# Holding back the first gates' sigmoids with a bias column made from the attention's last exponentials

## The chip, the cores and the metric

The kernel runs on one core of one Trainium2 chip. The metric is device time in microseconds (us), the median of the runs. Before the change it is 992.24 us, over three runs from 991.83 to 992.85 us.

## The reference

One layer of a streaming encoder, for 512 prompt frames and 32 frames of a running stream (544 columns in all, D_MODEL = 1024). What matters here is the stick-breaking attention, the gates, and what joins them:

```python
def stick_breaking_block(q, k, v, q_pos, k_pos):
    z = jnp.einsum('bqhd,bkhd->bhqk', q, k).astype(jnp.float32) * (SB_HEAD_DIM ** -0.5)
    mask = (k_pos[None, :] < q_pos[:, None])[None, None]
    u = jnp.where(mask, jax.nn.log_sigmoid(-z), 0.0)
    after = lax.cumsum(u, axis=3, reverse=True) - u
    w = jnp.where(mask, jnp.exp(jax.nn.log_sigmoid(z) + after), 0.0)
    return jnp.einsum('bhqk,bkhd->bqhd', w.astype(v.dtype), v)

def merge(o_ret, rg, o_sb, ga, gb, ret_norm_w_l, w_out_l):
    B, T = o_ret.shape[:2]
    r = rmsnorm(o_ret, ret_norm_w_l).reshape(B, T, RET_WIDTH).astype(rg.dtype) * jax.nn.silu(rg)
    s = o_sb.reshape(B, T, SB_WIDTH)
    mix = jax.nn.sigmoid(ga) * r + jax.nn.sigmoid(gb) * s
    return mix @ w_out_l
...
# rg, ga, gb are three of the nine parts of h @ w_in, h = rmsnorm(x)
# y = x + merge(...), then y + sq_relu_mlp(rmsnorm(y))
```

There are eight stick-breaking heads and four retention heads. The prompt's attention runs over all 512 frames; the sample's attention reads 512 cached keys and values beside its own 32.

## The kernel before, in words

Everything is held transposed: features on the 128 partitions, the 544 frames along the columns. Each float32 product is three products of rounded halves (hi x hi, lo x hi, hi x lo), made by `products` and `exact`. A projection (`gemm`) is a 128 x 1024 weight tile times the normalised input h, in two halves of 272 columns; a half is 24 matmuls into one PSUM bank of the pool `mm`, which has three banks. At its start `gemm` also calls `load_w`, which fetches the weight tile of the next one and splits it: a cast on ScalarE (ACT) to `whi`, a subtraction on VectorE (DVE) to `wlo`. There are two buffers of each, so the cast waits until the projection before this one has been read out of its weights.

The program first runs the heads in the order of `HEADS`, the last being stick-breaking heads S6 and S7, and then the gates: for each of the eight feature tiles t, the projections rg, ga and gb. Tile 0's three are only copied from PSUM (`first`, three `tmp` tiles). For t = 1 and later the sigmoid of rg is taken straight from PSUM (`silu`), then those of ga and gb. `first_mix`, called after the first projection of t = 1 (the fourth gate tile), takes the sigmoids of tile 0 and mixes it.

Between the matmuls of the projections, TensorE (PE) runs the steps of the attention as they become ready. A planner written in Python (`Flow`) sets PE's order by hand: each chain is a generator (`sb_chain` for a stick-breaking head, `sample_chain` for the cached attention of four heads, and others) that yields what it needs next, and `flow.poll()` between matmuls steps a chain whose inputs are due by the planner's own estimate of ACT's and DVE's time. That estimate holds lengths of operations and nothing for the loading of function tables. Only PE's order is set so (`manual_schedule`); the order on ACT and DVE is chosen by the framework's scheduler from what is ready in its own view.

One stick-breaking head does this: PE makes the scores in three banks (1280 packed columns); ACT takes Abs from PSUM into `e`, then Exp and Ln of `e` in place (softplus); DVE adds max(z, 0) and makes the halves `sh` (hi) and `sl` (lo) of the 1280 columns, then sums later blocks in `e` and makes three more 128-column pieces of `sh` (casts on ACT) and `sl` (DVE), in `later_parts`. PE subtracts the suffix sums from the scores (products of `sh` and `sl` with `tri_r` and `neg1_r`, shown as neg_r); ACT takes Exp of the result into `e`; DVE splits it, and PE multiplies by the values. The sample chain does the same for the sample with a scan on DVE in place of the triangular products; its last exponential is `cum`.

ACT has its functions in table sets, and an ACT_TABLE_LOAD stands in its order where the set changes. The program begins with a set that has both exp and ln. Sigmoid lies in another set. Where the scheduler lets a sigmoid in between two of the attention's functions, a load goes ahead of the sigmoid and another ahead of what follows; as the program is built, an Exp and an Ln that follow a sigmoid get a load each.

Of the kernel before, what the change touches and what calls it, by code (L numbers as in the profile page):

```python
# [9 lines left out]
F32 = mybir.dt.float32  # L10
F32R = mybir.dt.float32r
BF16 = mybir.dt.bfloat16
AF = mybir.ActivationFunctionType
ALU = mybir.AluOpType
# [10 lines left out]
NSB = 8  # L25
# [3 lines left out]
P = 128  # L29
# [3 lines left out]
PACKED = 1280  # L33
# [168 lines left out]
def need(*events, **parts):  # L202
    return events, parts
# [32 lines left out]
def trunk(ctx: ExitStack, tc: tile.TileContext, a: dict, g32):  # L236
    nc = tc.nc
    flow = Flow(mm=3, at=5, tmp=13, e=2, sh=1, qk0=1, qk1=1, qk2=1, qk3=1, vt=2, rv=1, rk=1, rq=1)
    V, S, T = (Timed(e, n, flow) for e, n in ((nc.vector, "V"), (nc.scalar, "S"), (nc.tensor, "T")))
# [97 lines left out]
    nc.vector.tensor_copy(ones_r, ones)  # L337
    ones = ones_r.bitcast(F32)
    ident = cst[:, C_ID:C_MP]
    epsb = const.tile([P, 1], F32, tag="epsb", name="epsb")  # L340
    nc.vector.memset(epsb, EPS)

# [51 lines left out]
    H = (h_hi, h_lo)  # L394
# [311 lines left out]
    def sb_chain(h, vt):  # L706
        yield need(("qk", h, 0), ("qk", h, 1), at=3, e=1)
        q_r, k_r = heads.pop((h, 0)), heads.pop((h, 1))
        z = [bank() for i in range(3)]
        e = bigp.tile([P, PACKED], F32, tag="e", name="e", bufs=2)  # L710
        for i in (0, 2):
            T.matmul(z[i][:, :P], id_b, mp_b, start=True, stop=False, **SG)
        T.matmul(
            z[1].rearrange("p (n c) -> p n c", c=P)[:, ::3, :], id_b,
            mp_b.rearrange("p (o c) -> p o c", o=1).to_broadcast([P, 2, P]), start=True, stop=False, **SG,
        )
        for bi, blocks in enumerate(GROUPS):
            for n, b in enumerate(blocks):
                _, c0, w = PIECES[b]
                by_blocks(z[bi][:, c0 : c0 + w], b, k_r, q_r, False, True)  # L720
        flow.give(qk0=1, qk1=1)
        for bi, (o, w) in enumerate(BANKS):
            S.activation(e[:, o : o + w], z[bi][:, :w], AF.Abs)
        S.activation(e, e, AF.Exp, scale=-1.0)
        S.activation(e, e, AF.Ln, bias=1.0)
        for bi, (o, w) in enumerate(BANKS):
            V.scalar_tensor_tensor(
                e[:, o : o + w], z[bi][:, :w], 0.0, e[:, o : o + w], op0=ALU.max, op1=ALU.add
            )
        yield need(sh=1)  # L730
        parts = packed_parts(e)
        later_parts(e, parts)
        yield need()
        for bi, blocks in enumerate(GROUPS):
            for b in blocks:
                bb, c0, w = PIECES[b]
                o = BANKS[bb][0] + c0
                own, later = z[bi][:, c0 : c0 + w], z[bi][:, c0 + P : c0 + w]
                if b == 3:
                    T.matmul(own, tri, e[:, o : o + w], start=False, stop=True, **SG)  # L740
                    continue
                for s in parts:
                    T.matmul(own, tri_r, s[:, o : o + w], start=False, stop=False, **SG)
                if b == 2:
                    T.matmul(later, neg1, e[:, 896:1024], start=False, stop=True, **SG)
                    continue
                for i, s in enumerate(parts):
                    T.matmul(
                        later.rearrange("p (n c) -> p n c", c=P), neg1_r, spaced(s, (512, 1024)[b], 3 - b),
                        start=False, stop=i == 1, **SG,  # L750
                    )
        flow.give(sh=1)
        for bi, (o, w) in enumerate(BANKS):
            S.activation(e[:, o : o + w], z[bi][:, :w], AF.Exp)
        flow.give(at=3)
        yield need(("v", h), sh=1, at=1)
        parts = packed_parts(e)
        yield need()
        ob = bank()
        values_of(ob, vt, slice(0, P), parts, e)  # L760
        S.copy(s_all[:, h, :SEQ], ob)
        flow.give(at=1, e=1, sh=1, vt=1)
        flow.finish("sb", h)

    def sample_chain(g):

        hs = range(4 * g, 4 * g + 4)
        yield need(*[("qk", h, i) for h in hs for i in range(2)], *[("v", h) for h in hs], tmp=6)
        kc, vc = [], []
        for h in hs:  # L770
            t = tmp()[:, :PAST]
            nc.gpsimd.dma_start(out=t, in_=a["kc"][h])
            kc.append(t)
        flow.t += 8000
        yield need(at=2)
        W0 = HT - DEC
        z = [bank(), bank()]
        T.matmul(z[0][:, :DEC], id_b, ms_b, start=True, stop=False, **SG)
        for j in range(4):
            T.matmul(z[0][j * DEC : (j + 1) * DEC, :DEC], qs[:, j, :], ks[:, j, :], start=False, stop=True, **SG)  # L780
        for j in range(4):
            T.matmul(
                z[0][j * DEC : (j + 1) * DEC, DEC:HT], qs[:, j, :], kc[j][:, :W0], start=False, stop=True, **SG
            )
        for j in range(4):
            T.matmul(z[1][j * DEC : (j + 1) * DEC, :HT], qs[:, j, :], kc[j][:, W0:], start=True, stop=True, **SG)
        for h in hs:
            t = tmp()[:, :PAST].rearrange("p (m e) -> p m e", m=4)
            nc.gpsimd.dma_start(out=t, in_=a["vc"][:, h * P : (h + 1) * P].rearrange("(m p) e -> p m e", p=P))
            vc.append(t)  # L790
        yield need()
        e, cum = tmp(), tmp()
        for i in range(2):
            S.activation(e[:, i * HT : (i + 1) * HT], z[i][:, :HT], AF.Abs)
        S.activation(e, e, AF.Exp, scale=-1.0)
        S.activation(e, e, AF.Ln, bias=1.0)
        for i in range(2):
            c = slice(i * HT, (i + 1) * HT)
            V.scalar_tensor_tensor(e[:, c], z[i][:, :HT], 0.0, e[:, c], op0=ALU.max, op1=ALU.add)
        V.tensor_tensor_scan(cum, ones[:, 0:1].to_broadcast([P, NT]), e, 0.0, op0=ALU.mult, op1=ALU.add)  # L800
        for i in range(2):
            c = slice(i * HT, (i + 1) * HT)
            V.tensor_tensor(cum[:, c], z[i][:, :HT], cum[:, c], op=ALU.subtract)
        flow.give(at=2)
        S.activation(cum, cum, AF.Exp)
        yield need(at=2)
        b = bank()
        for m in range(4):
            T.transpose(b[:, m * P : (m + 1) * P], cum[:, DEC + m * P : DEC + (m + 1) * P], ident)
        b2 = bank()  # L810
        T.transpose(b2[:DEC, :P], cum[:, :DEC], ident)
        wt = tp.tile([P, 4, P], F32, tag="tmp", name="wt")
        wn = sm.tile([DEC, P], F32, tag="wn", name="wn")
        S.copy(wt.rearrange("p m c -> p (m c)"), b)
        S.copy(wn, b2[:DEC, :P])
        flow.give(at=2)
        yield need(at=1)
        ob = bank()
        for m in range(5):
            for j in range(4):  # L820
                o = ob[j * DEC : (j + 1) * DEC, :P]
                if m < 4:
                    T.matmul(
                        o, wt[:, m, j * DEC : (j + 1) * DEC], vc[j][:, m, :], start=(m == 0), stop=False, **SG
                    )
                else:
                    T.matmul(o, wn[:, j * DEC : (j + 1) * DEC], vs[:, j, :], start=False, stop=True, **SG)
        flow.finish("sample", g)
        os_ = sm.tile([P, P], F32, tag="os", name="os")
        S.copy(os_, ob[:, :P])  # L830
        flow.give(at=1, tmp=6)
        yield need(at=1)
        b = bank()
        T.transpose(b[:, :P], os_, ident)
        V.tensor_copy(s_all[:, 4 * g : 4 * g + 4, SEQ:], b[:, :P].rearrange("p (h i) -> p h i", h=4))
        flow.give(at=1)
# [244 lines left out]
    def first_mix():  # L1081
        flow.wait(tmp=1)
        g, sa, sb = first
        sg = tmp()
        S.activation(sg, g, AF.Sigmoid)
        V.tensor_tensor(g, g, sg, op=ALU.mult)
        S.activation(sa, sa, AF.Sigmoid)
        V.tensor_tensor(g, g, sa, op=ALU.mult)
        V.tensor_tensor(g, g, r_all[:, 0, :], op=ALU.mult)
        S.activation(sb, sb, AF.Sigmoid)  # L1090
        V.tensor_tensor(sb, sb, s_all[:, 0, :], op=ALU.mult)
        V.tensor_tensor(g, g, sb, op=ALU.add)
        flow.give(tmp=3)
        held.append((0, g))

    for t in range(1, KD):
# [4 lines left out]
            S.activation(sg[:, c], p, AF.Sigmoid)  # L1101
            V.tensor_tensor(g[:, c], p, sg[:, c], op=ALU.mult)

        gemm(H, silu)
        flow.give(tmp=1)
        if t == 1:
            first_mix()
        flow.wait(tmp=1)
        sa = tmp()
        gemm(H, lambda h, c, p: S.activation(sa[:, c], p, AF.Sigmoid))  # L1110
# [397 lines left out]
```

## Time and profile before

| | |
|---|---|
| median of three runs | 992.24 us (991.83 to 992.85) |
| the profiled execution's own time | 993.84 us |
| its span in the trace | 992.1 us |
| PE busy | 982.7 us, 99% of the span |
| DVE busy | 667.6 us, 67% |
| ACT busy | 534.3 us, 54%, of which 13 ACT_TABLE_LOADs of 1.283 us |
| chain of waits that ended last | PE 97%, ACT 1%, DMA 1%, DVE 1% |

The span is the time between the first and the last instruction that the profiler saw; the execution's own time is 1.7 us more. Times of rows below are microseconds from the span's start. A matmul's duration in the trace overlaps the next one's: what one costs on PE is the distance from its start to the start of the next.

### The profile page before, as it was taken

The numbers are of one execution on the slowest core, as the hardware profiler recorded it, in microseconds if no ns is written. First come the engines' busy times: TensorE is split into PE (matmuls) and PEld (weight loads), VectorE is DVE, ScalarE is ACT, GpSimd is POOL, SyncE is SP. The second block draws the span as 40 slices with busy tenths as digits, with TensorE's granted clock in tenths as the row PEclk, the third lists the DMA queues.
The fourth block names the chain that finished last, engine by engine and source line by source line (L and its number), as shares of the span: only waits on it lengthen the run. The fifth ranks groups of instructions, "written<-read, shape, count | busy, mean of one in ns | idle before, by whom it ended". The sixth has DMA issues, their size and how long they took to land.

```text
span 992.1 us, 18727 instructions
## 1 busy us (share of the span) xinstructions
PE 982.7 (99%) x7766; PEld 968.9 (98%) x7766; DVE 667.6 (67%) x1127; ACT 534.3 (54%) x984; POOL 45.7 (5%) x80
## 2 busy tenths in 40 slices
PE   9999999999999999999999999999999999999998
PEld 9999999999999999988999999999999999999998
DVE  7987874787577756656644357975676666676782
ACT  6457554855576456777433345765464454444440
POOL 0001000120010001110000011000000000000000
PEclk9999999999999999999999999999999999999999
DMA  6233222352133212432422245232323323332312
GB/s 236 92 111 107 98 69 70 110 171 81 39 129 108 64 47 105 134 103 89 133 96 89 86 164 165 92 102 86 106 90 104 106 87 107 93 123 97 120 47 88
DMA packets 30933, 102.73 MB, mean 104 GB/s; under 512 B 4096, under 2 KB 6144, under 8 KB 30848
## 3 DMA queue, kind: packets, MB, share of 16 engines
q1 hardware_dynamic: 24768, 80.88, 25.1%
q0 software_dynamic: 6080, 20.65, 6.1%
q8 instruction: 61, 1.00, 0.4%
q14 instruction: 24, 0.20, 0.1%
HBM read 90.51 MB, written 11.01 MB: 102 GB/s over the span
## 4 chain that ended last, share of the span: by engine, by line
PE 97%; ACT 1%; DMA 1%; DVE 1%; issue 0%; SPq 0%; ACTq 0%; DVEq 0%
PE mm L229 71%; PE at L229 26%; DMA x<-in_x 1%; ACT L229 0%; ACT e L229 0%; ACT whi L229 0%; ACT tmp L229 0%; PE at L614 0%; DVE sl L229 0%; DVE tmp L229 0%; DVE wlo L229 0%; DVE e L229 0%; DVE sh L229 0%; ACT sh L229 0%; DVE x L229 0%
## 5 line engine op out<-in xcount | busy, mean ns | idle before, releaser
L229 PE MATMUL mm<-h_hi,whi 128*128 128x272 f32 x1040 | 303.4, 292 | 0.0
L229 PE MATMUL mm<-h_hi,wlo 128*128 128x272 f32 x1040 | 300.2, 289 | 0.0
L229 PE MATMUL mm<-h_lo,whi 128*128 128x272 f32 x1040 | 299.6, 288 | 0.0
L229 DVE TENSOR_TENSOR wlo<-raw,whi 128x1024 fp32r<-128x1024 f32 (+1 forms) x146 | 167.7, 1150 | 121.7 <-ACT whi L229 121.4
L229 ACT CAST whi<-raw 128x1024 fp32r<-128x1024 f32 (+1 forms) x146 | 144.6, 991 | 178.5 <-PE mm L229 158.2
L229 PEld LDWEIGHTS mm<-h_hi,whi 128*128 128x128 f32 x1040 | 196.1, 189 | 1.1 <-issue 0.6
L229 PEld LDWEIGHTS mm<-h_lo,whi 128*128 128x128 f32 x1040 | 196.2, 189 | 0.2
L229 PEld LDWEIGHTS mm<-h_hi,wlo 128*128 128x128 f32 x1040 | 195.6, 188 | 0.0
L229 PE MATMUL mm<-u_hi,whi 128*128 128x272 f32 x512 | 147.8, 289 | 0.0
L229 PE MATMUL mm<-u_lo,whi 128*128 128x272 f32 x512 | 147.7, 288 | 0.0
L229 PE MATMUL mm<-u_hi,wlo 128*128 128x272 f32 x512 | 147.6, 288 | 0.0
L229 PEld LDWEIGHTS mm<-u_hi,whi 128*128 128x128 f32 x512 | 96.5, 188 | 0.4 <-DVE y L229 0.2
L229 PEld LDWEIGHTS mm<-u_lo,whi 128*128 128x128 f32 x512 | 96.4, 188 | 0.0
L229 PEld LDWEIGHTS mm<-u_hi,wlo 128*128 128x128 f32 x512 | 96.2, 188 | 0.0
L229 ACT ACTIVATE tmp<-tmp 128x544 f32<-128x544 f32 (+2 forms) x157 | 80.6, 558 | 27.5 <-DVE tmp L229 27.0
L229 PE MATMUL at<-f_hi,wlo 128*128 128x272 f32 x320 | 92.6, 289 | 0.0
L229 PE MATMUL at<-f_lo,whi 128*128 128x272 f32 x320 | 92.1, 288 | 0.0
L229 PE MATMUL at<-f_hi,whi 128*128 128x272 f32 x320 | 92.1, 288 | 0.0
L229 DVE TENSOR_TENSOR y<-mm,y 128x272 f32<-128x272 f32 x112 | 48.7, 437 | 29.4 <-PE mm L229 29.4
L229 PEld LDWEIGHTS at<-f_hi,whi 128*128 128x128 f32 x320 | 60.5, 189 | 0.0
L229 PEld LDWEIGHTS at<-f_lo,whi 128*128 128x128 f32 x320 | 60.3, 188 | 0.0
L229 PEld LDWEIGHTS at<-f_hi,wlo 128*128 128x128 f32 x320 | 60.3, 188 | 0.0
(244 smaller groups left out, 1808.8 us busy)
## 6 DMA issues: line engine op xcount, KB each, us to landing
raw<-in_w SPq DMA_DIRECT2D x142, 512.0 KB, 3.5
x<-in_x SPq DMA_DIRECT2D x8, 272.0 KB, 6.0
o_v<-tmp POOLq DMA_DIRECT2D x8, 272.0 KB, 2.4
o_k<-tmp POOLq DMA_DIRECT2D x8, 272.0 KB, 2.4
x<-in_x POOLq DMA_DIRECT2D x8, 272.0 KB, 5.1
o_y<-x POOLq DMA_DIRECT2D x8, 272.0 KB, 2.9
tmp<-o_y POOLq DMA_DIRECT2D x8, 272.0 KB, 4.5
o_y<-y SPq DMA_DIRECT2D x16, 136.0 KB, 1.7
```

What stands on the lines that cost most here:

```text
L229: f(out, *args, **kw)
```

## The change

A const tile `late` of three columns is added. The last head's final exponentials (`e`) and the second sample chain's final exponential (`cum`) are each followed by a one-column DVE operation that multiplies a column of them by zero (columns 0 and 1 of `late`). `first_mix` and a new branch for t = 1 use column 2, the sum of both, as the bias of four sigmoids: it adds zero to what they compute, and makes them wait for both exponentials. For t = 1 the first projection, the fourth gate tile, is copied from PSUM and not put through the sigmoid there; the sigmoid is then taken from the copy over all 544 columns.

```diff
@@ -753,6 +755,9 @@
         for bi, (o, w) in enumerate(BANKS):
             S.activation(e[:, o : o + w], z[bi][:, :w], AF.Exp)
         flow.give(at=3)
+        if h == NSB - 1:
+            V.tensor_scalar(late[:, 0:1], e[:, PACKED - 1 :], 0.0, None, op0=ALU.mult)
+            flow.finish("late", 0)
         yield need(("v", h), sh=1, at=1)
         parts = packed_parts(e)
         yield need()
@@ -803,6 +808,9 @@
             V.tensor_tensor(cum[:, c], z[i][:, :HT], cum[:, c], op=ALU.subtract)
         flow.give(at=2)
         S.activation(cum, cum, AF.Exp)
+        if g == 1:
+            V.tensor_scalar(late[:, 1:2], cum[:, 0:1], 0.0, None, op0=ALU.mult)
+            flow.finish("late", 1)
         yield need(at=2)
         b = bank()
         for m in range(4):
@@ -1082,12 +1090,12 @@
         flow.wait(tmp=1)
         g, sa, sb = first
         sg = tmp()
-        S.activation(sg, g, AF.Sigmoid)
+        S.activation(sg, g, AF.Sigmoid, bias=late[:, 2:3])
         V.tensor_tensor(g, g, sg, op=ALU.mult)
-        S.activation(sa, sa, AF.Sigmoid)
+        S.activation(sa, sa, AF.Sigmoid, bias=late[:, 2:3])
         V.tensor_tensor(g, g, sa, op=ALU.mult)
         V.tensor_tensor(g, g, r_all[:, 0, :], op=ALU.mult)
-        S.activation(sb, sb, AF.Sigmoid)
+        S.activation(sb, sb, AF.Sigmoid, bias=late[:, 2:3])
         V.tensor_tensor(sb, sb, s_all[:, 0, :], op=ALU.mult)
         V.tensor_tensor(g, g, sb, op=ALU.add)
         flow.give(tmp=3)
@@ -1101,10 +1109,17 @@
             S.activation(sg[:, c], p, AF.Sigmoid)
             V.tensor_tensor(g[:, c], p, sg[:, c], op=ALU.mult)
 
-        gemm(H, silu)
+        if t == 1:
+            gemm(H, lambda h, c, p: S.copy(g[:, c], p))
+            flow.until("late", 0)
+            flow.until("late", 1)
+            V.tensor_tensor(late[:, 2:3], late[:, 0:1], late[:, 1:2], op=ALU.add)
+            S.activation(sg, g, AF.Sigmoid, bias=late[:, 2:3])
+            V.tensor_tensor(g, g, sg, op=ALU.mult)
+            first_mix()
+        else:
+            gemm(H, silu)
         flow.give(tmp=1)
-        if t == 1:
-            first_mix()
         flow.wait(tmp=1)
         sa = tmp()
         gemm(H, lambda h, c, p: S.activation(sa[:, c], p, AF.Sigmoid))
```

What this does to ACT's order is seen in two places. The first is ACT from the last head's Abs (`e<-at`) through its Exp and Ln (`e<-e`) to the first gates; `tmp<-mm` as COPY is a gate kept as it is, as ACTIVATE a gate's sigmoid, `tmp<-tmp` here a sigmoid of a copied gate, `whi` the cast of a weight tile. Before:

```order
L229 ACTIVATE e<-at 128x512 x2
L229 ACTIVATE e<-at 128x256
L229 ACT_TABLE_LOAD
L229 ACTIVATE e<-e 128x1280
L229 COPY tmp<-mm 128x272
L229 ACT_TABLE_LOAD
L229 ACTIVATE e<-e 128x1280
L229 CAST whi<-raw 128x1024
L229 ACT_TABLE_LOAD
L229 ACTIVATE tmp<-tmp 128x544
L229 ACTIVATE tmp<-mm 128x272
L229 CAST whi<-raw 128x1024
```

The same place of ACT in the changed kernel, on to the three casts of `sh`:

```order
L229 ACTIVATE e<-at 128x512 x2
L229 ACTIVATE e<-at 128x256
L229 ACTIVATE e<-e 128x1280 x2
L229 CAST whi<-raw 128x1024
L229 COPY tmp<-mm 128x272 x2
L229 CAST sh<-e 128x128
L229 CAST whi<-raw 128x1024
L229 CAST sh<-e 128x128 x2
L229 ACTIVATE tmp<-at 128x272 x2
L229 COPY tmp<-mm 128x272
```

The three loads are gone, Exp and Ln follow each other, and the sigmoids have become copies.

The second place is ACT a little later, where the sample's Exp and Ln (`tmp<-tmp` between the `sh` casts and after), the last head's final Exp (`e<-at`) and the sample's last Exp stand among sigmoids. Before, from the first `sh` cast:

```order
L229 CAST sh<-e 128x128
L229 ACT_TABLE_LOAD
L229 ACTIVATE tmp<-tmp 128x544
L229 CAST sh<-e 128x128 x2
L229 ACT_TABLE_LOAD
L229 ACTIVATE tmp<-tmp 128x544
L229 ACT_TABLE_LOAD
L229 ACTIVATE e<-at 128x512
L229 ACT_TABLE_LOAD
L229 ACTIVATE tmp<-tmp 128x544
L229 ACT_TABLE_LOAD
L229 ACTIVATE e<-at 128x512
```

In the changed kernel, from the sample's Exp and Ln on:

```order
L229 ACTIVATE tmp<-tmp 128x544 x2
L229 ACTIVATE e<-at 128x512 x2
L229 ACTIVATE e<-at 128x256
L229 ACTIVATE tmp<-tmp 128x544
L229 ACT_TABLE_LOAD
L229 ACTIVATE tmp<-tmp,late 128x544 x4
L229 ACTIVATE tmp<-mm 128x272 x2
L229 CAST whi<-raw 128x1024
```

One load is left, ahead of the four sigmoids that read `late`; over the whole program ACT has four loads where it had thirteen.

The third place is DVE in the changed kernel, from the last two `sl` pieces of the last head to the mixing of the gates (`tmp<-ones_r,tmp` is the sample's scan):

```order
L229 TENSOR_TENSOR sl<-e,sh 128x128 x2
L229 SCALAR_TENSOR_TENSOR tmp<-at,tmp 128x272 x2
L229 SCALAR_TENSOR_TENSOR tmp<-ones_r,tmp 128x544
L229 TENSOR_SCALAR late<-e 128x1
L229 CAST sh<-e 128x1280
L229 TENSOR_TENSOR tmp<-at,tmp 128x272 x2
L229 TENSOR_TENSOR sl<-e,sh 128x1280
L229 TENSOR_SCALAR late<-tmp 128x1
L229 TENSOR_TENSOR late<-late 128x1
L229 TENSOR_TENSOR tmp<-tmp 128x544 x3
```

The three `late` operations are new; before, the mixing of tile 0 was spread between the sample's subtraction and the last head's `sh` and `sl`, and now all of it follows. On PE nothing changes up to the gate projections that follow the last head's triangular products; there the sample's five transposes stand nine matmuls earlier, and the last head's product with the values three matmuls earlier.

## Rows read from the trace of the kernel before

**Rows 1.** The page: busy time of PE with its neighbours, and the shares by engine of the chain that ended last.

```profile
PE 982.7 (99%) x7766; PEld 968.9 (98%) x7766; DVE 667.6 (67%) x1127; ACT 534.3 (54%) x984; POOL 45.7 (5%) x80
...
PE 97%; ACT 1%; DMA 1%; DVE 1%; issue 0%; SPq 0%; ACTq 0%; DVEq 0%
```

**Rows 2.** The view of waits for PE over the whole trace: who was waited for, us in total, how often, the longest. All its five rows.

```profile
PE at L229 <- ACT sh L229: 3.1, 1, 3.1
PE at L388 <- DVE ones_r L337: 1.3, 1, 1.3
PE at L229 <- DVE sl L229: 0.8, 1, 0.8
PE mm L229 <- DVE x L229: 0.3, 1, 0.3
PE mm L229 <- ACT whi L229: 0.2, 1, 0.2
```

**Rows 3.** The timeline of PE around the two waits: start, duration, what, and idle time before it. 441.96 is the fourth gate tile's last matmul, 443.27 the first triangular product of head S7, 451.14 the first matmul of the next projection.

```profile
441.96 0.29 PE L229 MATMUL mm<-h_hi,wlo 128*128 128x272 f32 x1
...
443.27 0.50 PE L229 MATMUL at<-sh,tri_r 128*128 128x512 f32 x1
444.55 0.50 PE L229 MATMUL at<-sl,tri_r 128*128 128x512 f32 x1 [0.78 <-DVE sl L229]
448.12 0.44 PE L229 MATMUL at<-sh,neg_r 128*128 128x384 f32 x1 [3.07 <-ACT sh L229]
448.46 0.69 PE L229 MATMUL at<-sl,neg_r 128*128 128x384 f32 x1
...
451.14 0.57 PE L229 MATMUL mm<-h_hi,whi 128*128 128x272 f32 x1
...
451.94 0.28 PE L229 MATMUL mm<-h_hi,whi 128*128 128x272 f32 x1
```

**Rows 4.** The same products of head S6, before the change, where PE waited for nothing: its first `sh` product, its fourth product, the first matmul of the projection behind, and the fourth instruction from that one.

```profile
417.92 0.40 PE L229 MATMUL at<-sh,tri_r 128*128 128x512 f32 x1
...
418.56 0.34 PE L229 MATMUL at<-sl,neg_r 128*128 128x384 f32 x1
...
419.92 0.37 PE L229 MATMUL mm<-h_hi,whi 128*128 128x272 f32 x1
...
420.37 0.68 PE L229 MATMUL at<-tmp_r,ones_r 128*128 128x272 f32 x4
```

**Rows 5.** The table of stretches, PE alone: stretch, its length, busy time and count, granted clock of TensorE (1.00 is 2.4 GHz, 0.50 is 1.2 GHz), DMA share, GB/s.

```profile
449.00:450.00 1.00, 1.00 (x5) 0.50 0.88 348
...
452.00:453.00 1.00, 1.00 (x10) 1.00 0.00 0
```

**Rows 6.** The timeline of ACT over the last head and the first gates; a row with no names is an ACT_TABLE_LOAD.

```profile
433.76 1.28 ACT L229 ACT_TABLE_LOAD   x1
...
436.65 1.28 ACT L229 ACT_TABLE_LOAD   x1
437.95 1.27 ACT L229 ACTIVATE e<-e 128x1280 f32<-128x1280 f32 x1
...
442.31 1.04 ACT L229 CAST whi<-raw 128x1024 fp32r<-128x1024 f32 x1
...
443.54 0.68 ACT L229 ACTIVATE tmp<-at 128x272 f32<-128x272 f32 x2
445.42 0.30 ACT L229 CAST sh<-e 128x128 fp32r<-128x128 f32 x1 [1.20 <-DVE e L229]
445.74 1.28 ACT L229 ACT_TABLE_LOAD   x1
447.03 0.66 ACT L229 ACTIVATE tmp<-tmp 128x544 f32<-128x544 f32 x1
447.59 0.48 ACT L229 CAST sh<-e 128x128 fp32r<-128x128 f32 x2
```

**Rows 7.** The timeline of DVE over the same stretch.

```profile
439.25 1.62 DVE L229 SCALAR_TENSOR_TENSOR e<-at,e 128x512 f32<-128x512 f32 x3 [10.65 <-ACT e L229]
440.79 1.22 DVE L229 TENSOR_TENSOR wlo<-raw,whi 128x1024 fp32r<-128x1024 f32 x1
441.92 0.82 DVE L229 CAST sh<-e 128x1280 fp32r<-128x1280 f32 x1
...
443.01 1.48 DVE L229 TENSOR_TENSOR sl<-e,sh 128x1280 fp32r<-128x1280 f32 x1
...
445.04 0.29 DVE L229 TENSOR_TENSOR e<-e 128x128 f32<-128x128 f32 x1
...
445.60 0.42 DVE L229 TENSOR_TENSOR e<-e 128x256 f32<-128x256 f32 x1
...
447.90 0.50 DVE L229 TENSOR_TENSOR sl<-e,sh 128x128 fp32r<-128x128 f32 x2 [0.55 <-ACT sh L229]
450.07 0.79 DVE L229 SCALAR_TENSOR_TENSOR tmp<-at,tmp 128x272 f32<-128x272 f32 x2 [1.67 <-ACT tmp L229]
450.90 1.29 DVE L229 TENSOR_TENSOR_SCAN tmp<-ones_r,tmp 128x544 f32<-128x544 f32 x1
```

**Rows 8.** From the chain that ended last, in order of time: start, us, what. The longest unbroken piece of projection matmuls.

```profile
466.68 109.66 PE mm L229 x872
```

**Rows 9.** One line's instructions: a DVE operation on one column (L565), min/median/max in ns.

```profile
L565 DVE TENSOR_SCALAR nw<-wv x1: 148/148/148, 2.7 to 2.7; 128x1 f32<-128x1 f32 x1
```

More of the change, by code (lines that the diff above doesn't have):

```diff
@@ L339, in trunk @@
     ident = cst[:, C_ID:C_MP]
+    late = const.tile([P, 3], F32, tag="late", name="late")
     epsb = const.tile([P, 1], F32, tag="epsb", name="epsb")
```

## The prediction

> **What bounds the kernel now.** The page first: PE is busy 99% of the span and carries 97% of the chain that ended last [rows 1]. So ACT's table loads are worth only what PE waits for them. The view of waits for PE has five rows, 5.7 us in all, and 3.9 of these are two waits [rows 2]. The timeline of PE puts both in one place, the triangular products of the last head, S7: the second product waits 0.78 us for DVE's `sl`, the third 3.07 us for ACT's `sh` casts [rows 3]. The other three waits (1.3, 0.3, 0.2 us) lie elsewhere and the change does not touch them.
>
> Behind the wait PE is slow as well. From 449 to 450 us the granted clock is 0.50, 1.2 GHz, and after 452 it is 1.00 again [rows 5]; the fall comes after a stretch of nearly 4.9 us, 443.27 to 448.12, in which PE ran two products [rows 3]. What the place costs is read best by start times. From S7's first product to the fourth projection matmul it is 451.94 - 443.27 = 8.67 us [rows 3]. For head S6, which waited for nothing, the same instructions take 420.37 - 417.92 = 2.45 us [rows 4]. So 6.22 us are lost there: by comparing 448.46 to 451.94 (3.48 us) with S6's 418.56 to 420.37 (1.81 us), 1.67 of them behind the fourth product's start to the slow clock, the rest nearly all to waiting.
>
> **What made PE wait.** ACT's timeline shows it [rows 6]. S7's Abs is done at 433.76. A load stands before Exp and another before Ln (433.76 and 436.65), with a copy of a gate in between, so Ln ends at 439.22; DVE then begins its max-add at 439.25 after an idle time of 10.65 us for which ACT is named [rows 7]. Later a third load (445.74) and the sample's Exp (447.03) stand between the first `sh` cast and the other two, and PE's third product starts 0.05 us after these end.
>
> **The change, part by part.** On ACT the order has 4 loads where it had 13; nine of 1.28 us are 11.5 us of ACT, nearly all of it off the path. Each step on the path I take again in the new order, with durations of before. PE's order is the same up to here, so 443.27 stands.
>
> 1. Exp and Ln follow each other from 433.76: two times 1.27 to 1.28 us, Ln ends at 436.3 instead of 439.2, 2.9 us earlier (two loads and the copy).
> 2. DVE's three max-adds then run 436.35 to 438.0 (1.62 us). The weight tile's `wlo` stands next; its cast runs on ACT from 436.3 and is done before DVE is free; 1.22 us, with the overlap of the row 1.13, so the cast of `sh` starts at 439.0. It takes 0.82, `sl` 1.48: `sl` is ready at 441.4. PE wants it at 443.50 (0.23 behind the first product, as in S6's rows: four products from 417.92 to 418.56). The wait of 0.78 us is gone.
> 3. DVE's adds of 128 and 256 columns (0.29, 0.42 us) end at 442.05 [rows 7]; the first `sh` cast runs on ACT by 442.05 as well.
> 4. Next on ACT, ahead of the other two `sh` casts, now stands the weight cast of the projection behind. It overwrites the weights of the fourth gate tile, whose last matmul starts at 441.96 and ends 0.29 later [rows 3]; before, this cast started at 442.31 [rows 6], and it can hardly start sooner now. It takes 1.04; by the rows' overlap the two `sh` casts run 443.26 to 443.74 (0.48). PE could start the third product at 443.73: 0.06 us of waiting in place of 3.07.
> 5. DVE has `wlo` of that same weight tile ahead of the last two `sl`: 443.37, and 1.13 later, 444.50, the two `sl` with 0.50 us. They end at 445.00. PE's fourth product, which could start at 443.97, starts at 445.06 (before, it started 0.06 behind them too: 448.40 and 448.46): 1.09 us. This is what is late next.
>
> So PE waits 1.15 us where it lost 6.22. The clock: the largest idle time left is about a microsecond in place of 0.78 and 3.07 with one product between, and the 0.3 and 0.2 us waits elsewhere cost no clock that I see. I take it that it stays at 1.00, and keep the other case as a rival. **Gain: 6.22 - 1.15 = 5.07 us.**
>
> What the Trainium skill says of a load is larger: "ScalarE: Activation LUTs", section "What ACT_TABLE_LOAD costs", gives 1283 ns and a drain of some 1380 ns for each switch. The first number is this trace's; the drain isn't seen, since Ln starts 0.02 us behind its load [rows 6]. By the page the two loads of step 1 would give back 5.3 us and not 2.6: Ln would end at 433.9, although it and Exp need 2.5 us from 433.76 on. The rows decide, and the sum above holds no drain.
>
> **What the change adds.** Three one-column operations on DVE: not in the trace in this place; the nearest row is 148 ns on one column [rows 9], the far end is the longest operation of that stretch, the scan with 1.29 us [rows 7]; below nothing is excluded, they are new work. I take 0.15 us. They matter only through the four sigmoids, which wait for their sum on ACT's in-order queue. Behind these four stand the sigmoid of the next projection's first half, which frees a PSUM bank, then a weight cast. From step 5 on: the sample's Abs, the copy of the fourth gate's second half and Exp and Ln end on ACT at about 446.0 (0.68; 0.4 for 272 columns, about half of the two Abs; two of 0.66); DVE's max-add 0.79, scan 1.29, one column, `sh` cast 0.82 and subtraction 0.79 end at 449.8; the last Exp at 450.5, the one load that is left at 451.8. The column sum stands on DVE behind `sl` (1.48) and one more small operation: 451.5, hidden by the load. Four sigmoids of 0.66 end at 454.5, that half's sigmoid takes 0.4, and the bank is free at 454.9. PE starts the next projection at 445.06 + (419.92 - 418.56) = 446.42, and wants that bank three halves later, the earliest at 446.42 + 72 x 0.1258 = 455.5 (109.66 us for 872 matmuls [rows 8]). So it is covered, by 0.6 us. If the small operations cost 1.29 us each the column comes at 455.0, the bank at 458.0, and PE waits 2.5 us: gain 2.6.
>
> The mixing of tile 0 ends later on DVE, but what it feeds is only read after all the gates, and the `tmp` tiles that the sample's cached values load into were released long before. Behind this place PE has 109.66 us without a break [rows 8] and loses nothing that was gained.
>
> The sum is made against the profiled execution: 993.84 - 5.07 = 988.77 us. That execution is 1.60 us above the median of its runs, 992.24; I forecast the median: 992.24 - 5.07 = **987.2 us**.
>
> **The rivals.**
>
> - *The clock falls all the same* (0.11). Against it: the idle time left is a third of the longest one before. For it: the trace shows one fall only, so it doesn't tell how little idle time is enough. Then the slow stretch costs about the 1.67 us that it cost behind the fourth product: gain 3.4, 988.8 us.
> - *The wait vanishes altogether* (0.06), if DVE or ACT gets to the last pieces sooner than step 4 and 5 say: gain 6.2, 986.0 us. Against it: the weight cast cannot start before PE has read the old weights.
> - *Nothing is won, since something else than the loads made PE wait* (0.07): the `sh` casts were late because of DVE's work between, and PE finds another late input: within 2 us of 992. For it: of the 9.15 us from the max-add to the last `sl` before (439.25 to 448.40) my steps still hold 8.65. Against it: both ends move with Ln's 2.9 us, and PE's products come at a fixed 443.27.
> - *Slower* (0.04): the four held sigmoids keep the PSUM bank. It decides from 455.5 on; every microsecond later is one lost, and the kernel is slower than before once the bank comes after 460.6, that is if DVE's queue from Ln to the column sum takes 11.2 us instead of 5.5. With 13.5 us the bank comes at 462.9, PE waits 7.4, and the time is 992.24 - 5.07 + 7.4 = 994.6 us. Against it: before, the same work from the sample's max-add on was never waited for.
>
> **How the numbers follow.** My own case has 0.72, at 986.6 to 987.9 us by 0.3 us in each of steps 4 and 5 and what the runs scatter. With the clock's case at 988.8 and the dear small operations at 989.7 above, and the vanished wait at 986.0 below, the range is 985.9 to 989.7. About 0.2%, 2 us, is what a measurement of this kernel can tell from no change. Faster by more than that: 0.72 + 0.11 + 0.06 = 0.89. Within it: 0.07. Slower: 0.04.
>
> **What the new profile would show.** Right: four ACT_TABLE_LOADs, none between S7's Abs and its Exp and Ln; DVE's max-add at about 436.3; no wait of PE for S7's second product, and one of about 1 us, for `sl` and not for `sh`, at the fourth; the next projection at 446.4 instead of 451.1, at a clock of 1.00; no wait for a PSUM bank near 455. Wrong: a clock of 0.50 behind S7's products, a wait of PE on an ACT sigmoid, or a max-add that starts as late as before although the loads are gone.

## The result and the profile after

The changed kernel takes 986.76 us, the median of four runs from 986.35 to 987.61. The kernel before took 992.04 us beside it (four runs, 991.74 to 992.85). The medians differ by 5.28 us. The ratio on record is 0.9942, with a 95% interval of 0.9929 to 0.9954 (the two medians alone give 0.9947). Of all runs behind this document one, of the kernel below in which the fourth gate tile isn't kept, took 1356.21 us at a mean granted clock of 0.657, and the ratios leave it out. The profiled execution's own time is 986.62 us, its span 984.9 us.

On the page, where [rows 1] stood before, ACT has lost 11 us of work and PE 3.8:

```profile
PE 978.9 (99%) x7766; PEld 965.6 (98%) x7766; DVE 667.8 (68%) x1129; ACT 523.3 (53%) x976; POOL 45.9 (5%) x80
...
PE 99%; DMA 0%; ACT 0%; DVE 0%; issue 0%; SPq 0%
```

The view of waits for PE, all its rows, answers to [rows 2]. The 3.1 us for `sh` is gone; one wait of 0.7 us for `sl` is left.

```profile
PE at L390 <- DVE ones_r L337: 1.3, 1, 1.3
PE at L229 <- DVE sl L229: 0.7, 1, 0.7
PE mm L229 <- ACT whi L229: 0.2, 1, 0.2
```

The timeline of PE at head S7's triangular products answers to [rows 3]. The columns are start, duration, what, and the idle time before it; the last line is the fourth matmul of the next projection.

```profile
441.89 0.50 PE L229 MATMUL at<-sh,tri_r 128*128 128x512 f32 x1
442.23 0.40 PE L229 MATMUL at<-sl,tri_r 128*128 128x512 f32 x1
442.46 0.34 PE L229 MATMUL at<-sh,neg_r 128*128 128x384 f32 x1
443.55 0.44 PE L229 MATMUL at<-sl,neg_r 128*128 128x384 f32 x1 [0.74 <-DVE sl L229]
...
445.02 0.37 PE L229 MATMUL mm<-h_hi,whi 128*128 128x272 f32 x1
...
445.48 0.29 PE L229 MATMUL mm<-h_hi,whi 128*128 128x272 f32 x1
```

From the first product to the fourth projection matmul this is 445.48 - 441.89 = 3.59 us, against 8.67 before: **5.08 us won in this place**. 3.53 of these are waiting ahead of the fourth product (448.46 - 443.27 = 5.19 us before, 1.66 now); the other 1.55 lie behind its start (3.48 us before, 1.93 now), where the clock was slow before. The first product itself starts 1.38 us earlier in this execution than in the one before, and that has nothing to do with the change (the last section has more on it). So the two profiled executions, 993.84 and 986.62, differ by 7.22 us: 5.08 here, 1.38 ahead of here, 0.54 at the wait on `x` that this execution did not have (three starts from 585.23 to 586.03 us before, the same three from 578.60 to 578.86 now), and some 0.2 that gathers slowly over the projections between, without a wait. The medians, which even out much of such chance, differ by 5.28.

ACT's timeline answers to [rows 6]. Exp and Ln are one row (x2), and one load stands behind the sample's last Exp, ahead of the four held sigmoids (`tmp<-tmp,late`):

```profile
432.40 2.58 ACT L229 ACTIVATE e<-e 128x1280 f32<-128x1280 f32 x2
...
440.79 1.05 ACT L229 CAST whi<-raw 128x1024 fp32r<-128x1024 f32 x1
441.74 0.49 ACT L229 CAST sh<-e 128x128 fp32r<-128x128 f32 x2
...
447.99 0.66 ACT L229 ACTIVATE tmp<-tmp 128x544 f32<-128x544 f32 x1 [1.82 <-DVE tmp L229]
448.67 1.28 ACT L229 ACT_TABLE_LOAD   x1
449.96 2.67 ACT L229 ACTIVATE tmp<-tmp,late 128x544 f32<-128x544 f32 x4
452.54 0.66 ACT L229 ACTIVATE tmp<-mm 128x272 f32<-128x272 f32 x2
```

DVE's timeline answers to [rows 7]. The max-add no longer waits 10.65 us but 7.74, and the one-column operations are the short rows with `late`:

```profile
435.01 1.62 DVE L229 SCALAR_TENSOR_TENSOR e<-at,e 128x512 f32<-128x512 f32 x3 [7.74 <-ACT e L229]
...
438.53 1.49 DVE L229 TENSOR_TENSOR sl<-e,sh 128x1280 fp32r<-128x1280 f32 x1
...
441.86 1.23 DVE L229 TENSOR_TENSOR wlo<-raw,whi 128x1024 fp32r<-128x1024 f32 x1 [0.80 <-ACT whi L229]
443.00 0.48 DVE L229 TENSOR_TENSOR sl<-e,sh 128x128 fp32r<-128x128 f32 x2
...
446.40 0.13 DVE L229 TENSOR_SCALAR late<-e 128x1 f32<-128x1 f32 x1
...
449.45 0.16 DVE L229 TENSOR_TENSOR late<-late 128x1 f32<-128x1 f32 x1
```

What is left of the wait reads straight off: DVE's `wlo` starts when ACT's `whi` is done, the last two `sl` stand behind it and start at 443.00, and PE's fourth product starts at 443.55.

### The profile page after: what moved, and what is told of

It reads as the page before. It is cut to its first block, busy times and chain, and to the rows that moved or that the text cites. A ratio compares the mean times of both kernels' runs of the same rounds, so it can differ in the third digit from the quotient of the medians.

```text
span 984.9 us, 18722 instructions
## 1 busy us (share of the span) xinstructions
PE 978.9 (99%) x7766; PEld 965.6 (98%) x7766; DVE 667.8 (68%) x1129; ACT 523.3 (53%) x976; POOL 45.9 (5%) x80
## 4 chain that ended last, share of the span: by engine, by line
PE 99%; DMA 0%; ACT 0%; DVE 0%; issue 0%; SPq 0%
PE mm L229 73%; PE at L229 26%; DMA x<-in_x 0%; ACT whi L229 0%; PE at L616 0%; ACT tmp L229 0%; DVE sl L229 0%; DVE y L229 0%; DVE wlo L229 0%; SPq L332 0%
## 5 line engine op out<-in xcount | busy, mean ns | idle before, releaser
L229 ACT ACTIVATE tmp<-tmp 128x544 f32<-128x544 f32 (+2 forms) x154 | 78.6, 556 | 29.2 <-DVE tmp L229 28.7
```

The source lines that it names most:

```text
L229: f(out, *args, **kw)
```

## The experiments

The theory: the gain is the two loads between S7's Abs, Exp and Ln and the third one between its `sh` casts, which PE waited for, and the slow clock behind that wait. The rivals: it is the gates' own work on ACT and DVE that got out of the way, whatever the loads; or any part of the change (the copies, the columns) does it alone. The first four kernels ran on one chip, beside the kernel before at 993.05 us there; the last three on one chip too, with the kernel before at 992.92.

**One sigmoid put back.** A one-column sigmoid before the last head's Abs makes Exp and Ln follow a sigmoid again. Its one-column result is overwritten by the Abs. Where an expectation speaks of S7's stretch, it means the time from S7's first product to the fourth projection matmul.

```diff
         flow.give(qk0=1, qk1=1)
+        if h == NSB - 1:
+            S.activation(e[:, 0:1], q_r[0][:, 0:1].bitcast(F32), AF.Sigmoid)
         for bi, (o, w) in enumerate(BANKS):
             S.activation(e[:, o : o + w], z[bi][:, :w], AF.Abs)
```

> The changed kernel with one more instruction: a sigmoid of a single column, ahead of the last head's Abs. The gates' sigmoids stay held back, but ACT's order has again a load before S7's Exp, one before its Ln, and one before the sample's Exp, between the sh casts. If the loads made PE wait (the loads' theory): Ln ends about 2.9 us later than in the changed kernel, PE waits about 0.8 us at S7's second product, 3 us at the third, and from S7's first product to the fourth projection matmul 8 to 8.7 us pass instead of 3.6; 4.5 to 5 us slower than the changed kernel, some 991.5 us, if the clock falls as it did before, and about 990 us if it doesn't. If it was the gates' own work on ACT and DVE in that stretch (the rival), which stays away here: within 1 us of 986.8.

Measured: 992.56 us (991.39 to 993.39, 11 runs), ratio to the kernel before 0.9997 (0.9988 to 1.0006). The whole gain is gone, and the median lies 1 us above what was expected. ACT's timeline of this kernel has the three loads in their old places, though the gates' sigmoids are still held:

```profile
432.47 1.28 ACT L229 ACT_TABLE_LOAD   x1
433.76 1.28 ACT L229 ACTIVATE e<-e 128x1280 f32<-128x1280 f32 x1
435.37 1.28 ACT L229 ACT_TABLE_LOAD   x1
...
443.41 0.30 ACT L229 CAST sh<-e 128x128 fp32r<-128x128 f32 x1 [1.20 <-DVE e L229]
...
444.29 1.28 ACT L229 ACT_TABLE_LOAD   x1
445.59 0.66 ACT L229 ACTIVATE tmp<-tmp 128x544 f32<-128x544 f32 x1
446.15 0.48 ACT L229 CAST sh<-e 128x128 fp32r<-128x128 f32 x2
```

PE's timeline has both waits, and the table of stretches for PE (stretch, length, busy time and count, granted clock, DMA share, GB/s) the slow clock behind them:

```profile
441.98 0.50 PE L229 MATMUL at<-sh,tri_r 128*128 128x512 f32 x1
443.05 0.49 PE L229 MATMUL at<-sl,tri_r 128*128 128x512 f32 x1 [0.57 <-DVE sl L229]
446.68 0.69 PE L229 MATMUL at<-sh,neg_r 128*128 128x384 f32 x1 [3.14 <-ACT sh L229]
...
450.26 0.29 PE L229 MATMUL mm<-h_hi,whi 128*128 128x272 f32 x1
```

```profile
448.00:449.00 1.00, 1.00 (x7) 0.50 0.00 0
```

8.28 us from the first product to the fourth projection matmul, 8.67 before and 3.59 in the changed kernel: 4.69 of the 5.08 us are lost again in this place. It is the loads, with the order that comes with them. Three more loads are back as well, ahead of the one-column sigmoid (426.39), of the sample's Ln (446.65) and of the last head's final Exp (448.62). These cost nothing: no wait of PE answers to them, and from the fourth projection matmul to the product that reads `os` (464.35 us here, 459.57 in the changed kernel) 14.09 us pass in both. The edit also moves what the scheduler puts beside the loads (the first `sh` cast is again a row of its own, with the sample's work behind it), as the loads did before, so it doesn't part the loads' own 1.28 us from the order that comes with them.

**The fourth gate tile not kept.** The three sigmoids of tile 0 stay held; the fourth gate tile's is taken from PSUM as before.

```diff
         if t == 1:
-            gemm(H, lambda h, c, p: S.copy(g[:, c], p))
+            gemm(H, silu)
...
-            S.activation(sg, g, AF.Sigmoid, bias=late[:, 2:3])
-            V.tensor_tensor(g, g, sg, op=ALU.mult)
             first_mix()
```

> The bias on the three sigmoids of tile 0 alone; the fourth gate tile is put through its sigmoid straight from PSUM, as before the change. ACT's order keeps S7's Exp and Ln together, but has loads again around the sample's Exp, Ln and last Exp, and a weight cast that waits for PE now stands ahead of the last Exp and the held sigmoids. If only the loads ahead of S7's products counted, and the kept fourth tile is idle: S7's stretch takes 3.6 to 4.0 us and the time is 986.5 to 987.5. If what comes behind counts too: the same stretch, but PE waits 2 us for the sample's last Exp at its transposes and 2 us for a PSUM bank, 3.5 to 5 us more than the changed kernel, 990 to 992 us.

Measured: 993.13 us (median of 11 runs, ten of them from 990.68 to 993.51), ratio 0.9999 (0.9990 to 1.0008). S7 is as good as in the changed kernel: 446.93 - 443.26 = 3.67 us. But the second sigmoid of the fourth tile now stands just ahead of the sample's Abs, Exp and Ln, so that the sample's Exp, Ln and last Exp get a load each, and the weight cast ahead of the last load waits for PE. ACT's timeline up to the sample's last Exp:

```profile
452.65 1.05 ACT L229 CAST whi<-raw 128x1024 fp32r<-128x1024 f32 x1 [2.92 <-PE mm L229]
453.72 1.28 ACT L229 ACT_TABLE_LOAD   x1
455.01 0.66 ACT L229 ACTIVATE tmp<-tmp 128x544 f32<-128x544 f32 x1
```

That Exp comes late, and PE has two new waits for ACT, all its rows over 0.5 us:

```profile
PE at L229 <- ACT tmp L229: 2.2, 1, 2.2
PE at L390 <- DVE ones_r L337: 1.3, 1, 1.3
PE at L229 <- DVE sl L229: 0.8, 1, 0.8
PE mm L229 <- ACT tmp L229: 0.6, 1, 0.6
```

Behind the wait of 2.2 us the granted clock falls, by the table of stretches for PE:

```profile
456.00:457.00 1.00, 1.00 (x7) 0.50 0.80 225
...
459.00:460.00 1.00, 1.00 (x8) 0.85 0.00 0
```

Two waits of 2.8 us together and about 3.4 us at half speed, another 1.7, give back 4.5 of the 5.1. The wait at the transposes was expected, at 2 us; the one for the bank is 0.6 and not 2, and the fall of the clock was not expected, so the time is 1 us over the range that was set down. So the kept tile is no trimming: without it the loads move to the sample's chain. Loads are not all of that chain's delay. The sample's subtraction on DVE ends 10.72 us after S7's first product (453.98 - 443.26), 6.07 in the changed kernel (447.96 - 441.89); two loads are 2.6 of these 4.65 us, and the rest is the order on ACT and DVE.

**No bias.** The copies, the columns and PE's order of the changed kernel, with nothing that holds the four sigmoids back.

```diff
-        S.activation(sg, g, AF.Sigmoid, bias=late[:, 2:3])
+        S.activation(sg, g, AF.Sigmoid)
...
-            S.activation(sg, g, AF.Sigmoid, bias=late[:, 2:3])
+            S.activation(sg, g, AF.Sigmoid)
```

(and likewise for `sa` and `sb` of tile 0.)

> The changed kernel without the bias on its four sigmoids: the fourth gate tile is still copied, the columns are still made, and PE's order is the changed kernel's. ACT's order has nearly all of its loads back. If the held sigmoids do the work: S7's stretch takes 8 to 9 us again and the time is 991 to 993 us, that of the kernel before. If the copy of the fourth tile or PE's new order did it: near 987 us.

Measured: 991.32 us (990.56 to 992.18, 11 runs), ratio 0.9978 (0.9969 to 0.9987). The 12 loads behind the program's first are back, and PE waits 1.08 us for `sl` and 1.83 for `sh`. The clock falls here too, behind the two waits:

```profile
444.26 0.49 PE L229 MATMUL at<-sl,tri_r 128*128 128x512 f32 x1 [1.08 <-DVE sl L229]
446.58 0.44 PE L229 MATMUL at<-sh,neg_r 128*128 128x384 f32 x1 [1.83 <-ACT sh L229]
```

```profile
449.00:450.00 1.00, 1.00 (x6) 0.50 0.00 0
```

The stretch takes 7.11 us, less than the 8 to 9 expected, but the slow clock reaches beyond its end, and up to the product that reads `os` 0.59 us more are lost (14.68 us, 14.09 in the changed kernel). That is 4.1 of the 5.1 us. So the copies, the columns and the order of PE carry about 1.0 us by the trace and 1.7 by the medians (1.3 to 3.1 by the interval), and the wait that the bias makes carries the rest.

**The last wait taken away, in three tries.** The 0.74 us left comes from `wlo` ahead of the last two `sl` on DVE. The first try holds that `wlo` behind the last `sl` (a column of ones made of it is multiplied in), and in the same manner the next `whi` cast behind the held sigmoids.

```diff
+            V.tensor_scalar(late[:, 3:4], parts[1].bitcast(F32)[:, 1280:1281], 0.0, 1.0, op0=ALU.mult, op1=ALU.add)
...
+            S.activation(hi, src, AF.Copy, scale=hold)
+            V.scalar_tensor_tensor(lo, src, one, hi.bitcast(F32), op0=ALU.mult, op1=ALU.subtract)
```

> The changed kernel, with two more columns: the subtraction that makes wlo of the weight tile behind S7 is scaled by a column of ones made from the last sl pieces, and the next weight cast by one made from a held sigmoid. It tries to take away what is late next in the changed kernel. If wlo ahead of the last two sl is what PE's fourth product waits for: its wait falls from about 1.0 to 0.2 us, no wait appears for a PSUM bank, and the time is 0.8 us less, 986.0 us, which a median hardly tells. If the wait has another cause: unchanged, 986.8 us; if holding the casts costs more than it gives: a wait of PE behind 450 us and over 987.5.

Measured: 987.88 us (986.54 to 989.07, 5 runs), ratio 0.9946 (0.9933 to 0.9958): no better than the change, and the last of the three outcomes that were set down. The stretch is 2.64 us and its wait is gone; PE waits in another place instead, by the view of waits and the timeline of ACT:

```profile
PE mm L229 <- ACT tmp L229: 1.0, 1, 1.0
```

```profile
449.38 0.66 ACT L229 ACTIVATE tmp<-tmp 128x544 f32<-128x544 f32 x1 [4.23 <-DVE tmp L229]
450.06 1.28 ACT L229 ACT_TABLE_LOAD   x1
451.36 2.67 ACT L229 ACTIVATE tmp<-tmp,late 128x544 f32<-128x544 f32 x4
453.93 0.66 ACT L229 ACTIVATE tmp<-mm 128x272 f32<-128x272 f32 x2
```

DVE now takes the last head's `sh` cast ahead of the sample's scan and its `sl` ahead of the sample's subtraction, the sample's last Exp comes at 449.38, the load and the held sigmoids behind it, and the PSUM bank that the last row reads comes free too late.

The second try, `wlo` held alone, was run with the changed kernel itself beside it. In these expectations both_held is the first try and after_again the changed kernel run once more; the seventh sub-block's products, and the eighth sub-block's exponentials and value products in the third try, all belong to head S7; the prefix sum is the sample's scan.

> The changed kernel unaltered, beside the two below on the same chip. Theory (the gain is a fixed piece of the path, about 5.1 us at the seventh sub-block's products): ratio to the kernel before 0.9945 to 0.9953, first product to fourth projection matmul 3.6 us at granted clock 1.00, a wait of 0.7 for the last `sl`. Rival (part of the 5.3 us between the medians is the length of the slow start of the program, which has nothing to do with the change): the medians differ by under 4.5 us here.

> The changed kernel with the `wlo` subtraction of the following weight tile held behind the last `sl` alone; the next `whi` cast isn't held. Theory (the wait of 0.7 for `sl` goes, but the `whi` cast now stands ahead of the load and the held sigmoids, so that the PSUM bank comes free 1 us later than in both_held): a wait of 1.5 to 2.2 us of PE for the bank, and 0.6 to 1.2 us over after_again. Rival (the bank has 1.8 us to spare in the changed kernel, so a cast of 1.05 ahead costs nothing): 0.7 to 0.9 us under after_again, with no wait for the bank.

Measured: the changed kernel 986.51 us (985.42 to 988.21, 5 runs), ratio 0.9939 (0.9927 to 0.9952). The stretch of 3.58 us and the wait of 0.75 came as expected; the ratio lies just below the range of 0.9945 to 0.9953, which the interval overlaps. The rival, under 4.5 us between the medians, did not come, since they differ by 6.4 here; but that is 1.3 more than the 5.1 in the trace, and where these lie is not known. With `wlo` held alone: 989.41 us (988.30 to 990.92, 6 runs), ratio 0.9972 (0.9960 to 0.9984). The wait for the bank is there, in the timeline of PE:

```profile
456.02 0.39 PE L229 MATMUL mm<-h_hi,whi 128*128 128x272 f32 x1 [1.93 <-ACT tmp L229]
```

1.93 us with a `whi` cast of 1.03 more ahead of the load, 0.99 without it: the cast's length shows nearly one for one. Set against the 0.94 us won at S7 this is a loss of 1.0 us, within the expected 0.6 to 1.2; but the medians differ by 2.9. The profiled execution does not hold the rest: its clock stays at 1.00 behind that wait, and its time, 988.30, is the lowest of the six. The mean granted clock of the single executions points to where it is. It is 1.000 in this one and one other (989.39), and 0.998 in the other four (988.69 to 990.92), as in the profiled executions of the kernel before and of the three experiments above in which the clock fell; the changed kernel has 0.999 or 1.000. So in most executions the clock seems to fall with this wait as well, for 1.7 us more, what the fall behind S7 cost. That it falls in this place is not shown, since none of the four was profiled.

The third try holds the last head's `sh` cast on DVE as well, behind the sample's subtraction:

```diff
+            V.tensor_scalar(hi[:, :PACKED], x, one, None, op0=ALU.mult)
...
+            V.tensor_scalar(late[:, 5:6], cum[:, 0:1], 0.0, 1.0, op0=ALU.mult, op1=ALU.add)
```

> both_held, and the DVE cast of the eighth sub-block's exponentials to `sh` is held by a column of ones made of the sample's subtraction, so that the prefix sum and the subtraction stand ahead of it. Theory (the 1.0 wait for the PSUM bank in both_held came from the sample's last Exp, late at 449.38 because that cast stood ahead of the prefix sum): the Exp starts near 447.4, the load near 448.1, the bank is read by 452.4, the wait for it goes, first product to fourth projection matmul stays at 2.6 us; 0.9 to 1.0 us under after_again. Rival (the work only moves, and another wait takes the place of this one, at the transposes or at the eighth sub-block's value products, whose `sl` now ends about 2 us later): the same time as after_again within 0.3 us, with a new row of 0.7 us or more among PE's waits.

Measured: 986.30 us (985.38 to 986.87, 5 runs), ratio 0.9935 (0.9923 to 0.9948): level with the changed kernel. The theory's steps came, but not its 0.9 to 1.0 us: the sample's last Exp at 446.90, no wait for the bank, a stretch of 2.65 us. But ACT's load is followed by 0.70 us of idle time for the column sum, since on DVE `sl` stands ahead of it, and PE, whose order the planner changed as well, waits for the transposed weights of the sample that ACT copies behind all this:

```profile
454.36 1.08 PE L229 MATMUL at<-tmp,wt 128*32 128x128 f32 x32 [0.77 <-ACT wt L229]
```

The rival stands: 0.77 us in place of 0.74. No version tried here beats the changed kernel by more than the runs scatter.

## Why the prediction was right, step by step

The forecast was 987.2 us and a gain of 5.07; measured were 986.76, 5.08 in the trace and 5.28 between the medians. To set the two traces side by side, 1.38 us is added to the times of the new one.

- *Steps 1 and 2, the loads ahead of the max-add.* The max-add was forecast for 436.35 and comes at 436.39 (435.01). `sl` was to be ready at 441.4: it starts at 439.91 and takes 1.49, so 441.40. The wait of 0.78 us is gone. The one-sigmoid run, which puts these loads and the third back (and three that PE does not wait for), gives back the whole gain.
- *Steps 3 and 4, the `sh` casts.* They were to end at 443.74 and end at 443.61 (441.74 + 0.49). The weight cast stands ahead of them, as read from the order, and starts 0.14 us sooner than forecast. The third product has no wait in its row, where 0.06 was forecast.
- *Step 5, what is late next.* The last two `sl` end at 444.86 (443.00 + 0.48), forecast 445.00; the fourth product starts at 444.93, forecast 445.06. From the first product to the fourth is 1.66 us, where S6 took 0.64 [rows 4]: 1.02 us of waiting, for `sl`, where 1.15 was forecast. (The row's 0.74 is less, since it counts from the modelled end of the product before.) From the fourth product on, PE takes 1.93 us to the fourth projection matmul, S6 1.81. So 1.14 us of the 6.22 are left: the sum was right to 0.01 by a miss of 0.13 on the wait and one of 0.12 behind it, which cancel.
- *The clock.* It was taken to stay at 1.00, and does. The next projection, forecast for 446.4, starts at 446.40 (445.02), and the stretch below, in the new trace's own time, lies within it:

```profile
446.00:447.00 1.00, 1.00 (x11) 1.00 0.02 8
```

 This was the step with the least behind it, as the trace had one fall only. The traces of the experiments add three: the clock falls with waits of 0.57 and 3.14 close together (one sigmoid put back), with 1.08 and 1.83 (no bias) and with one of 2.23 (fourth tile not kept). It holds in the traces with single waits of 0.74, 0.77, 0.99 and 1.93. The same waits don't always end the same way, though: with the 1.93, four of six executions have a mean of 0.998, as told above, and two of the eleven without the bias have 1.000. The changed kernel's nine executions all have 0.999 or 1.000.
- *What the change adds.* The small operations cost 0.13 to 0.16 us; 0.15 was taken from the nearest row [rows 9]. The sum is ready at 449.6, and the load in front of the sigmoids ends at 449.95, so it is hidden as forecast.
- *The rival on the slower side.* It did not come here: the bank is read by 452.9 and wanted at 454.69 (the 73rd matmul of that projection), 1.8 us later where 0.6 was forecast. The forecast had left out the sample's transposes between those matmuls and had ACT 0.6 us slower. But its mechanism is real: two experiments in which the held sigmoids start 1.9 and 2.9 us later after S7's first product made PE wait for just this bank, and lost what they had won or more.
- *Four loads* are left, as forecast (the program's first, and three behind), and ACT's 11.0 us less on the page answer to nine loads, 11.5 us. Three of the nine, 3.85 us, stood where PE waited for what came behind them; the rest of the 5.08 is the order that came with them and the slow clock.

The step on the drain also stands. The Trainium skill ("ScalarE: Activation LUTs", section "What ACT_TABLE_LOAD costs") adds some 1380 ns of drain to a load's 1283 ns. Here the load ends at 449.95 and the sigmoids start at 449.96, and the Exp ahead of it ends within 0.02 us of its start; an estimate by that page's two figures for Exp's and Ln's loads, 5.3 us, is well over the 2.9 by which the max-add came earlier.

## What to carry to other kernels

Count a table load where a scheduler that prices none puts it between two functions of one set: here the loads cost what the readers of their neighbours' results waited, plus the slow clock behind a long wait, and nothing elsewhere. An operand of zeros made of the last value that must come first is a cheap way to keep an operation back (0.15 us here), but everything that must not pass between has to be held too, and everything that the held operations keep (a PSUM bank here) must have time to spare. With 1 us left on this path, moving one operation more only handed the wait to another queue: the change left 0.74 us of waiting for `sl`, and the three tries 0.99 and 1.93 for a PSUM bank and 0.77 for the sample's weights.

## What the runs showed that was not expected

The program's first 15 us don't take the same time from one execution to the next, and the granted clock does not tell it. In the table of stretches, the kernel before has 6 matmuls in a microsecond at a granted clock of 1.00:

```profile
14.00:15.00 1.00, 1.00 (x6) 1.00 1.02 428
```

and the changed kernel, which runs the same instructions there, 10:

```profile
14.00:15.00 1.00, 1.00 (x10) 1.00 0.98 412
```

S7's first product starts anywhere from 440.79 to 443.27 us in the nine traces, and at 441.89 and 442.31 in the two of the changed kernel. The starts of the matmuls say more than the table. In the kernel before, matmuls of 272 columns start every 0.23 us up to 14.89, and every 0.13 from 15.06 on; in the changed kernel the step comes at 12.57. Behind S7 their distance is 0.23 as well where the granted clock is 0.50 (451.51 to 451.74), and 0.13 at 1.00. So the early pace is that of the lower level, though the table gives 1.00. The DMA share doesn't part the two: from 13 to 14 us it is 1.09 with 7 matmuls before and 1.07 with 10 after. What sets the step was not tried. The 2.5 us by which it comes sooner are an estimated 1.1 of the 1.38 us that lie ahead of S7's first product. For the reading of such a change it means that a cost is taken between two starts within one trace, and not from the difference of two spans.
